# A hybrid attention and linear-attention decoder step: one pass reordered by output column, ACT's results stored from ACT's queue, split weights stored later, one more raw weight slot, bias set-up four steps sooner

## The chip, the cores and the metric

The kernel runs on one core of a Trainium2 chip. The metric is the device time of one execution in microseconds. The engines are named as in the profile: PE multiplies matrices (PEld is its weight load), DVE, ACT and POOL do elementwise work, and SP here does nothing but issue DMAs. ACT and POOL can issue DMAs too. Each engine works through its own queue in order; a wait in a queue holds everything behind it.

## The reference

One layer of a decoder works on 2048 prompt tokens and 64 sample tokens (8 sequences of 8), with a model width of 1024. All data are float32.

```
z = x @ w_in                      # 1024 -> q, k, v, g_att, gq, gk, gv, g_gla, g_lr, r_att, r_gla
o_att = windowed attention(q, k, v) with sinks and a relative bias       # 8 heads, window 128
o_gla = gated linear attention(gq, gk, gv, log_sigmoid(g_lr @ w_gk_up + b_gk))   # 4 heads, chunks of 64
h_att = (o_att * silu(g_att)) @ w_pa          # 512 -> 1024
h_gla = (rmsnorm(o_gla) * silu(g_gla)) @ w_pg # 1024 -> 1024
merged = sigmoid(r_att) * h_att + sigmoid(r_gla) * h_gla
x = layer_norm(ALPHA * x + merged @ w_o)
```

It also returns the last K and V rows and the linear-attention states.

## The kernel before

**Three products for one.** A float32 product is made of three fast ones: each operand is split into a rounded high part and the rest (`split`: ACT casts the high part at L142, DVE subtracts at L143), and PE adds high*high (L1291), high*low (L1292) and low*high (L1293).

**Sets, passes, groups.** The 2112 tokens are cut into three blocks of 704, each of two halves of T = 352. The work of PE is a fixed list of 719 `groups`, in nine sets: x0 (groups 0 to 176), x1 (177 to 351), a0, u0, x2, a1, u1, a2, u2. A set "x" multiplies the input of one token block by all columns of `w_in`; a set "a" is attention's projection `w_pa` (32 groups), a set "u" the projection `w_pg` (32 groups). A pass is a weight with 256 output columns (p); two passes go side by side (j = 0, 1). In the sets x a pass is done by a seven-product scheme on 2x2 blocks (`ORDER`), with sums and differences of weight blocks made by POOL (`tt`, L338). In the sets a and u (`PLAIN`) it is done plainly: a group is `(c, k, t)` for the output column block c, the depth block k and the token half t. A group with `kh` = 4 is 12 matmuls of 128x352, one with `kh` = 2 (the sets a) is 6. The products of the two k of one (c, t) add up in one PSUM bank; with k = 1 the bank is complete and its sink reads it. Four banks (`role`) take turns.

**Weights.** Three helpers run ahead of PE by a number of groups. `w_first` (LR = 8 ahead) has SP load a raw block into a slot of the ring `ws` (9 slots). `w_make` (LM = 4 ahead) has POOL combine blocks where the scheme asks for it, and ACT and DVE split them into a slot of the ring `wp` (6 slots). In x0 four of seven split weights are then stored by SP in DRAM (`wk_d`, L361), and `w_kept` (LK = 5) loads them back in x1 and x2.

**Sinks.** `combine` hands each finished block to the pass's sink. `keep_sink` stores q, k and v (where the block is still in PSUM, ACT copies it first, L186); `silu_sink` the gates; `tanh_sink` (the passes w_ra and w_rg at the end of each set x) has ACT take a tanh (L211) and SP store it (L212); `gated_sink` (sets a) has DVE multiply a block with its gate (L219), which `partners` had SP load (L175, LP = 2 groups ahead), and SP store it (L221). All these tiles come from the ring `fin` (10 slots).

**Side work.** Attention (`att_*`), the linear attention (`gla_*`), the low-rank gate (`gate`, L703) and the set-up of the relative bias (`setup0` to `setup5`) are put between the groups by `at(t, f)`: f is emitted after group t's work, counted in steps of one full group. In this version the bias set-up starts at step 17, its products (`setup1`) come at steps 20, 22, 24 and 26, and the two calls of `gate` in x0 come at steps 22 and 26. `setup3` loads the bias for each phase of attention by eight DMAs (L669).

**Order.** PE's order is the order in which the code emits (a manual schedule). On the other engines a scheduler orders the instructions, except where `issue_after` pins one behind another; so an engine may run ahead of the group list.

Of the kernel before, what the change touches and what calls it, by code (L numbers as in the profile page):

```python
# [12 lines left out]
F32 = mybir.dt.float32  # L13
# [8 lines left out]
P = 128  # L22
# [35 lines left out]
def kernel(ctx, tc, io):  # L58
# [20 lines left out]
    T = MT  # L79

    def mtile(tag, dt=F32, name=None):
        n, bufs = {"xb": (4 * T, 16), "a": (T, 8), "fin": (T, 10), "ws": (512, 9), "wp": (D, 6)}[tag]
        pool = px if tag == "xb" else pr
        return pool.tile([P, n], dt, tag=tag, name=name or tag, bufs=bufs)

# [38 lines left out]
    def at(t, fn):  # L124
        side.setdefault(max(int(t), now[0]), []).append(fn)
# [24 lines left out]
    def later(f):  # L150
        def g():
            with tc.issue_after(pin["a"].ins), tc.issue_after(pin["d"].ins):
                f()
        return g
# [27 lines left out]
    def keep_sink(dst):  # L182
        def f(z, ps, parts, p, c, ts):
            if ps:
                z, src = mtile("fin"), z
                nc.scalar.copy(z, src)  # L186
            nc.sync.dma_start(dst[:, c, ts], z)
            wrote(dst, c, ts)
        return f

# [15 lines left out]
    def tanh_sink(dst):  # L206
        def f(z, ps, parts, p, c, ts):
            src = z
            if ps:
                z = mtile("fin")  # L210
            nc.scalar.activation(z, src, AF.Tanh, scale=0.5)  # L211
            nc.sync.dma_start(dst(2 * p + c, ts), z)  # L212
        return f

    def gated_sink(z, ps, parts, p, c, ts):
# [41 lines left out]
    for n, (kind, s, kh, prs) in enumerate(sets):  # L257
        start_of.append(len(groups))
        base.append(int(tk))
        for pr_ in prs:  # L260
            if not groups:
                for k, t in ((0, 0), (1, 0), (0, 1), (1, 1)):
                    for c in range(2):
                        for j, (q, p) in enumerate(pr_):
                            groups.append((n, q, (c, k, t), s, p, 4 * t + 2 * c + j, False))
            elif seq[n] in PLAIN:
                for c in range(2):
                    for k in range(2):
                        for j, (q, p) in enumerate(pr_):
                            for t in range(2):  # L270
                                groups.append((n, q, (c, k, t), s, p, role[2 * j + t], False))
            elif len(pr_) == 2:
                for i in ORDER:
                    for j, (q, p) in enumerate(pr_):
                        b = role[j] if i in (1, 6, 5, 3) else role[2 + j]
                        groups.append((n, q, i, s, p, b, True))
                role = role[2:] + role[:2]
            else:
                (q, p), = pr_
                r = [role[2], role[3], role[0], role[1]]  # L280
                for j, i in enumerate(ORDER):
                    groups.append((n, q, i, s, p, r[j % 4], False))
                role = [r[3], r[0], r[1], r[2]]
        tk += (len(groups) - start_of[-1]) * kh / 4
# [3 lines left out]
    XS = (X0, X1, X2)  # L288


    raws, wps, acc, parts = {}, {}, {}, {}
    LR, LK, LM, LP = 8, 5, 4, 2
    BLK = {1: (0, 0), 7: (1, 0), 6: (1, 1), 2: (0, 1)}

    def made_here(q, p, s):
# [5 lines left out]
    def w_first(g):  # L301
        n, q, i, s, p, b, ch = groups[g]
        if type(i) is tuple:
            c = None if i[2] else i[:2]
        elif made_here(q, p, s):
            c = BLK.get(i)
        else:
            c = None if i in KEPT else {1: (0, 0), 2: (0, 1), 4: (1, 1)}[i]
        if c is not None:
            t = mtile("ws")[:, :q.kh * P]  # L310
            nc.sync.dma_start(t, q.w[c[0], c[1], p])
            raws[q.name, p, c] = t

    def w_kept(g):
# [5 lines left out]
    def w_make(g):  # L320
# [37 lines left out]
        split(w[:, :m], w[:, m:], src)  # L358
        if i in KEPT and keeps(q, p, s):
            d = wk_d[q.name, p, i] = dram.tile([P, 2 * m], F32, name=f"wk_{q.name}{p}{i}")  # L360
            nc.sync.dma_start(d, w.bitcast(F32))  # L361

    def combine(g, ps):
        n, q, i, s, p, b, ch = groups[g]
# [245 lines left out]

    nbgk = const.tile([P, GH], F32, name="nbgk")
    wgk = const.tile([P, HK], F32, name="wgk")
    at(8, later(consts))

    sink = const.tile([P, NH], F32, name="sink")
# [47 lines left out]
    def setup3():  # L663
        flat = bs_d.rearrange("h q j -> h (q j)")
        for kv in range(2):
            b = w4(name="bias").rearrange("p (g k) -> p g k", g=G)
            for g in range(G):
                f = flat[kv * G + g, 127:127 + P * (LB - 1)].rearrange("(q j) -> q j", j=LB - 1)
                nc.sync.dma_start(b[:, g, :], f[:, :2 * W])  # L669
            st1["bias", kv] = b  # L670

    bias_s = const.tile([P, 2, W + TS], F32, name="bias_s")
# [10 lines left out]
            nc.sync.dma_start(bias_s[32 * b:32 * b + 32], bias_s[:32])  # L683


    at(17, later(setup0))
    for h in range(0, NH, 2):
        at(20 + h, later(lambda h=h: setup1(h)))
    at(20, later(setup2))
    at(29, later(setup4))  # L690
    at(34, setup5)

    def gate_load(B):
        x = B["x"] = mtile("fin", name="gin")
# [124 lines left out]
    def samp_load():  # L819
        for z in [z_kv] + z_q + z_ga:  # L820
            need(z, range(2), NP, NT)
        SA["kv"] = mt("skv", 2 * NS, 1).rearrange("p (a t) -> p a t", a=2)
        SA["kw"] = mt("kw", W, 1)
        nc.sync.dma_start(SA["kv"], z_kv[:, :, NP:])
        nc.sync.dma_start(SA["kw"], z_kv[:, 0, NP - W:NP])
        SA["zq"], SA["sil"] = (mt("zs", G * W, 4, name=n)[:, :G * NS].rearrange("p (g t) -> p g t", g=G) for n in ("szq", "ssl"))
        for j in range(2):
            nc.sync.dma_start(SA["zq"][:, 2 * j:2 * j + 2], z_q[j][:, :, NP:])
            nc.sync.dma_start(SA["sil"][:, 2 * j:2 * j + 2], z_ga[j][:, :, NP:])
        kc = w4(name="kc").rearrange("p (b c) -> p b c", b=NB)  # L830
        vc = w4(name="vc").rearrange("p (b c) -> p b c", b=NB)
        nc.sync.dma_start(kc, io["ck"].rearrange("b w c -> w b c"))
        nc.sync.dma_start(vc, io["cv"].rearrange("b w c -> w b c"))
        SA["kc"], SA["vc"] = kc, vc
        nc.sync.dma_start(io["o_ks"][:, 0:W - TS, :], io["ck"][:, TS:W, :])
        nc.sync.dma_start(io["o_vs"][:, 0:W - TS, :], io["cv"][:, TS:W, :])
# [277 lines left out]
    def samp_a(B):  # L1114
# [7 lines left out]
        nc.gpsimd.memset(qz, 0.0)  # L1122
        for b in range(NB):
            nc.vector.tensor_copy(qz[:, b, b % 4 * TS:(b % 4 + 1) * TS], B["q"][:, Tp + b * TS:Tp + (b + 1) * TS])
        kz = mt("kz", 4 * HK, 1).rearrange("p (b k) -> p b k", b=4)
        nc.vector.tensor_tensor(kz, kdT.unsqueeze(1).broadcast_to([P, 4, HK]),
                                bsel.unsqueeze(2).broadcast_to([P, 4, HK]), ALU.mult)
        B.update(qz=qz, kz=kz)
# [135 lines left out]

    wo = []
    half = 0
    last_ = start_of[U2] + 14
    NG = len(groups)
    for g, (n, q, i, s, p, b, ch) in enumerate(groups):
        if 8 <= g + LR < NG:  # L1270
            w_first(g + LR)
        if g + LK < NG:
            w_kept(g + LK)
        if 8 <= g + LM < NG:
            w_make(g + LM)
        if g + LP < NG:
            _, q_, i_, s_, p_, _, _ = groups[g + LP]
            parts[g + LP] = q_.partners(i_, p_, s_)
        xh, xl = ops[n].op[i[1:] if type(i) is tuple else i]
        w = wps.pop(g)  # L1280
        m = q.kh * P
# [267 lines left out]
```

## Time and profile before

| | |
|---|---|
| three runs | 1844.45, 1842.92, 1842.38 us, median 1842.92 us |
| profiled execution | 1844.21 us, its span 1842.3 us |
| PE busy | 1782.9 us, 97% of the span |
| DVE, ACT, POOL busy | 1062.9 us (58%), 832.6 us (45%), 336.1 us (18%) |
| mean granted TensorE clock | 0.99 |
| data moved | 452.03 MB, 245 GB/s |

PE's busy share says that PE is nearly always at work; what is left is found by cutting the span into stretches and looking at each for PE's idle time and for the granted clock, which falls to half for some microseconds after some of the stalls. The wait lists say on what PE waited, and SP's own list says what the DMAs behind it waited for.

### The profile page before, as it was taken

The page shows a single profiled execution, that of the slowest core. Times are in us where ns is not written, and L with a number is a line of the kernel's source. Part 1 is how long each engine was busy: PE and PEld are TensorE (multiplying, and loading weights), DVE is VectorE, ACT ScalarE, POOL GpSimd, SP SyncE. Part 2 cuts the span into 40 slices and gives each one's busy share as a digit, 9 for nine tenths or more (in the row PEclk, how much of TensorE's full clock was granted, in tenths as well). Part 3 has the DMA queues.
Part 4 walks back from the last instruction along what each step waited for, and adds up shares of the span by engine and source line. Part 5 has one row for each costly group of instructions (what it writes and reads, how often), then busy time and mean ns, then how long its engine had stood idle before and what let it go on. Part 6 is the DMA issues. An engine that isn't in the chain of part 4 may idle for free.

```text
span 1842.3 us, 31141 instructions
## 1 busy us (share of the span) xinstructions
PE 1782.9 (97%) x10850; PEld 1659.2 (90%) x10850; DVE 1062.9 (58%) x2077; ACT 832.6 (45%) x1983; POOL 336.1 (18%) x473
## 2 busy tenths in 40 slices
PE   8989999998999999999899999999999999999997
PEld 7888988998898899999899998899999889998886
DVE  6568676767636554545566446545455544535665
ACT  5747554645835643545334645544445332311100
POOL 4333345454100000000033000000000022021111
PEclk9999999999999999999999999999999999999999
DMA  6689588887698779888886897689888987976531
GB/s 192 237 294 320 196 291 284 299 281 244 201 297 290 239 233 295 274 262 270 285 236 134 274 313 228 218 277 330 264 279 284 299 228 188 293 152 213 159 110 52
DMA packets 291340, 452.03 MB, mean 245 GB/s; under 512 B 29981, under 2 KB 210517, under 8 KB 291168
## 3 DMA queue, kind: packets, MB, share of 16 engines
q1 hardware_dynamic: 283264, 440.61, 72.6%
q0 software_dynamic: 7824, 9.31, 3.6%
q8 instruction: 86, 1.41, 0.3%
q14 instruction: 70, 0.57, 0.1%
q10 hardware_dynamic: 96, 0.13, 0.0%
HBM read 297.52 MB, written 153.30 MB: 245 GB/s over the span
## 4 chain that ended last, share of the span: by engine, by line
PE 71%; DMA 11%; ACT 6%; DVE 5%; issue 3%; POOL 3%; SPq 1%; DVEq 0%; ACTq 0%; POOLq 0%
PE pd L1291 16%; PE pd L1293 16%; PE pd L1292 16%; PE pd L1355 3%; PE pd L1354 3%; PE pd L1356 3%; DMA ws<-w_g 2%; POOL ws L338 2%; DMA r<-ug_d 2%; DVE wp L143 1%; DMA part<-ra_d 1%; PE pa L811 1%; PE pa L765 1%; PE pa L797 1%; PE pa L1085 1%
## 5 line engine op out<-in xcount | busy, mean ns | idle before, releaser
L143 DVE TENSOR_TENSOR wp<-ws,wp 128x512 fp32r<-128x512 f32 (+1 forms) x396 | 271.9, 691 | 216.4 <-ACT wp L142 207.8
L142 ACT CAST wp<-ws 128x512 fp32r<-128x512 f32 (+1 forms) x396 | 233.7, 595 | 222.0 <-PE pd L1293 145.0
L338 POOL TENSOR_TENSOR ws<-ws 128x256 f32<-128x256 f32 x162 | 140.6, 898 | 159.9 <-DVE wp L143 116.0
L1071 POOL TENSOR_SCALAR sq<-sq 128x1 f32<-128x1 f32 x68 | 22.6, 333 | 727.6 <-ACT on L1070 727.6
L374 ACT COPY m<-pd 128x352 f32<-128x352 f32 x146 | 65.6, 453 | 89.2 <-PE pd L1293 89.1
L1291 PE MATMUL pd<-x7h,wp 128*128 128x352 f32 x292 | 97.4, 334 | 4.0 <-ACT wp L142 2.4
L1355 PE MATMUL pd<-woh,x 128*128 128x512 f32 x256 | 100.0, 391 | 0.0
L1354 PE MATMUL pd<-woh,x 128*128 128x512 f32 x256 | 99.8, 390 | 0.0
L1356 PE MATMUL pd<-wol,x 128*128 128x512 f32 x256 | 99.5, 389 | 0.0
L1291 PE MATMUL pd<-x1h,wp 128*128 128x352 f32 x292 | 96.2, 329 | 2.9 <-ACT fin L186 2.3
L1291 PE MATMUL pd<-x2h,wp 128*128 128x352 f32 x292 | 98.7, 338 | 0.0
L1291 PE MATMUL pd<-x6h,wp 128*128 128x352 f32 x292 | 97.5, 334 | 0.9 <-ACT wp L142 0.9
L1291 PE MATMUL pd<-x3h,wp 128*128 128x352 f32 x292 | 97.1, 333 | 0.0
L1291 PE MATMUL pd<-x4h,wp 128*128 128x352 f32 x292 | 96.9, 332 | 0.0
L1291 PE MATMUL pd<-x5h,wp 128*128 128x352 f32 x292 | 96.9, 332 | 0.0
L1293 PE MATMUL pd<-x1h,wp 128*128 128x352 f32 x292 | 94.3, 323 | 1.8 <-DVE wp L143 1.8
L1293 PE MATMUL pd<-x7h,wp 128*128 128x352 f32 x292 | 94.4, 323 | 0.9 <-DVE wp L143 0.7
L1292 PE MATMUL pd<-x2l,wp 128*128 128x352 f32 x292 | 95.0, 325 | 0.0
L1293 PE MATMUL pd<-x5h,wp 128*128 128x352 f32 x292 | 94.9, 325 | 0.0
L1292 PE MATMUL pd<-x5l,wp 128*128 128x352 f32 x292 | 94.9, 325 | 0.0
L1293 PE MATMUL pd<-x2h,wp 128*128 128x352 f32 x292 | 94.7, 324 | 0.0
L1293 PE MATMUL pd<-x6h,wp 128*128 128x352 f32 x292 | 94.4, 323 | 0.1
(441 smaller groups left out, 5271.0 us busy)
## 6 DMA issues: line engine op xcount, KB each, us to landing
wp<-wk_w_g SPq DMA_DIRECT2D x96, 512.0 KB
ws<-w_g SPq DMA_DIRECT2D x120, 256.0 KB
wk_w_g<-wp SPq DMA_DIRECT2D x48, 512.0 KB
wp<-wk_w_ra SPq DMA_DIRECT2D x32, 512.0 KB
wp<-wk_w_rg SPq DMA_DIRECT2D x32, 512.0 KB
ws<-w_at SPq DMA_DIRECT2D x54, 256.0 KB
wp<-wk_w_at SPq DMA_DIRECT2D x24, 512.0 KB
ws<-w_pg SPq DMA_DIRECT2D x48, 256.0 KB
```

Source lines behind the costliest of these rows:

```text
L142: pin["a"] = nc.scalar.copy(dst_h, src)
L143: i = eng.tensor_tensor(dst_l, src, dst_h.bitcast(F32), ALU.subtract)
L338: nc.gpsimd.tensor_tensor(o[:, c], x[:, c], y[:, c], op)
L374: nc.scalar.copy(A[i], ps)
L765: mm(ps[kv][:, j, k0:], A["zq"][r, g0 + j, :], A["kk"][r, 0, k0:], start=True, stop=True, tile_position=(kv * HD, 0))
L1071: nc.gpsimd.tensor_scalar(sq[:n], sq[:n], EPS, None, op0=ALU.add)
L1291: mm(ps, wh, xh[:, ts], start=first, stop=False, skip_group_check=ch)
L1292: mm(ps, wh, xl[:, ts], start=False, stop=False, skip_group_check=ch)
L1293: mm(ps, wl, xh[:, ts], start=False, stop=(k == q.kh - 1 and not (type(i) is tuple and i[1] == 0)), skip_group_check=ch)
L1354: mm(ps, xh[:, xs], hi, start=(k == 0), stop=False)
L1355: mm(ps, xl[:, xs], hi, start=False, stop=False)
L1356: mm(ps, xh[:, xs], lo, start=False, stop=(k == KT - 1))
```

## The change

- **Order of the sets a.** Within one column block c, the pass j is now outside the depth block k: a pass's two k follow each other, four groups to a pass, and its two banks are read while the other pass is at work. The sets u keep their order.
- **Queues.** The stores that follow an ACT instruction (`tanh_sink` always, `keep_sink` where ACT copied from PSUM) are issued from ACT's queue and no longer from SP's.
- **Split weights.** A store of a split weight is emitted one group later and pinned behind the newest raw load on SP.
- **Lead.** One more `ws` slot (10) and one group more of lead for raw loads (LR = 9); in x0 one group more for splitting (LM + 1); for the gates of the sets a four groups more (LP + 4).
- **Space.** One slot fewer for the scheme's intermediate sums (`a`, 7); three tiles of the sample work move into the rings `fin` and `ws`.
- **Bias set-up.** All its steps come four steps sooner (`SU` = 13), and `setup3` loads with one DMA for four heads: two instead of eight.

```diff
-        n, bufs = {"xb": (4 * T, 16), "a": (T, 8), "fin": (T, 10), "ws": (512, 9), "wp": (D, 6)}[tag]
+        n, bufs = {"xb": (4 * T, 16), "a": (T, 7), "fin": (T, 10), "ws": (512, 10), "wp": (D, 6)}[tag]
...
-            nc.sync.dma_start(dst[:, c, ts], z)
+            (nc.scalar if ps else nc.sync).dma_start(dst[:, c, ts], z)
...
             nc.scalar.activation(z, src, AF.Tanh, scale=0.5)
-            nc.sync.dma_start(dst(2 * p + c, ts), z)
+            nc.scalar.dma_start(dst(2 * p + c, ts), z)
...
+                jk = [(j, k) for j in range(2) for k in range(2)]
                 for c in range(2):
-                    for k in range(2):
-                        for j, (q, p) in enumerate(pr_):
-                            for t in range(2):
-                                groups.append((n, q, (c, k, t), s, p, role[2 * j + t], False))
+                    for j, k in jk if kind == "a" else [(j, k) for k, j in jk]:
+                        q, p = pr_[j]
+                        for t in range(2):
+                            groups.append((n, q, (c, k, t), s, p, role[2 * j + t], False))
...
-    LR, LK, LM, LP = 8, 5, 4, 2
+    LR, LK, LM, LP = 9, 5, 4, 2
...
-            nc.sync.dma_start(t, q.w[c[0], c[1], p])
+            pin["r"] = nc.sync.dma_start(t, q.w[c[0], c[1], p])
...
             d = wk_d[q.name, p, i] = dram.tile([P, 2 * m], F32, name=f"wk_{q.name}{p}{i}")
-            nc.sync.dma_start(d, w.bitcast(F32))
+            late.setdefault(g - 3, []).append(lambda: nc.sync.dma_start(d, w.bitcast(F32)))
...
+    SU = 13
...
-            for g in range(G):
-                f = flat[kv * G + g, 127:127 + P * (LB - 1)].rearrange("(q j) -> q j", j=LB - 1)
-                nc.sync.dma_start(b[:, g, :], f[:, :2 * W])
+            f = flat[kv * G:(kv + 1) * G, 127:127 + P * (LB - 1)].rearrange("g (q j) -> q g j", j=LB - 1)
+            nc.sync.dma_start(b, f[:, :, :2 * W])
...
-    at(17, later(setup0))
+    at(SU, later(setup0))
     for h in range(0, NH, 2):
-        at(20 + h, later(lambda h=h: setup1(h)))
-    at(20, later(setup2))
-    at(29, later(setup4))
-    at(34, setup5)
+        at(SU + 3 + h, later(lambda h=h: setup1(h)))
+    at(SU + 3, later(setup2))
+    at(SU + 12, later(setup4))
+    at(SU + 17, setup5)
...
-        SA["kv"] = mt("skv", 2 * NS, 1).rearrange("p (a t) -> p a t", a=2)
-        SA["kw"] = mt("kw", W, 1)
+        SA["kv"] = mtile("fin", name="skv")[:, :2 * NS].rearrange("p (a t) -> p a t", a=2)
+        SA["kw"] = mtile("fin", name="kw")[:, :W]
...
-        kz = mt("kz", 4 * HK, 1).rearrange("p (b k) -> p b k", b=4)
+        kz = mtile("ws", name="kz").rearrange("p (b k) -> p b k", b=4)
...
-        if 8 <= g + LM < NG:
-            w_make(g + LM)
-        if g + LP < NG:
-            _, q_, i_, s_, p_, _, _ = groups[g + LP]
-            parts[g + LP] = q_.partners(i_, p_, s_)
+        while nm < NG and nm <= g + (LM + 1 if groups[nm][3] == 0 and seq[groups[nm][0]] == "x0" else LM):
+            w_make(nm)
+            nm += 1
+        for f in late.pop(g, ()):
+            with tc.issue_after(pin["r"].ins):
+                f()
+        while nq < NG and nq <= g + (LP + 4 if groups[nq][1] is PA_ else LP):
+            _, q_, i_, s_, p_, _, _ = groups[nq]
+            parts[nq] = q_.partners(i_, p_, s_)
+            nq += 1
```

More of the change, by code (lines that the diff above doesn't have):

```diff
@@ L288 @@
     XS = (X0, X1, X2)
-    raws, wps, acc, parts = {}, {}, {}, {}
-    LR, LK, LM, LP = 8, 5, 4, 2
+    raws, wps, acc, parts, late = {}, {}, {}, {}, {}
+    LR, LK, LM, LP = 9, 5, 4, 2
     BLK = {1: (0, 0), 7: (1, 0), 6: (1, 1), 2: (0, 1)}
@@ L1266 @@
     half = 0
-    last_ = start_of[U2] + 14
+    nm, nq = 8, 0
     NG = len(groups)
```

## The prediction

> **What bounds the kernel now.** I read the page first, then the span in stretches, then PE's waits, then SP's own waits, and last the timeline at the stalls.
>
> ```profile
> PE 1782.9 (97%) x10850; PEld 1659.2 (90%) x10850; DVE 1062.9 (58%) x2077; ACT 832.6 (45%) x1983; POOL 336.1 (18%) x473
> ...
> PE 71%; DMA 11%; ACT 6%; DVE 5%; issue 3%; POOL 3%; SPq 1%; DVEq 0%; ACTq 0%; POOLq 0%
> ```
>
> PE is the bound, and the change removes no PE instruction. What it can win is PE's idle time and the time at a low clock. The stretches, cut at the borders of the sets, show where these lie (length, then busy time and instructions of PE, PEld, DVE, ACT, POOL, then clock, DMA share, GB/s):
>
> ```profile
> 0.00:40.00 40.00, 32.84 (x180) 31.45 (x180) 23.09 (x33) 20.63 (x35) 22.08 (x40) 1.00 0.67 214
> 40.00:100.00 60.00, 57.72 (x320) 48.65 (x321) 36.85 (x55) 41.34 (x83) 16.30 (x20) 0.91 0.62 217
> 100.00:135.00 35.00, 29.69 (x190) 26.84 (x189) 20.98 (x42) 16.48 (x45) 13.22 (x16) 1.00 0.91 309
> ...
> 232.00:302.00 70.00, 64.25 (x394) 61.69 (x393) 51.82 (x92) 37.36 (x88) 33.80 (x43) 1.00 0.81 279
> 302.00:400.00 98.00, 93.45 (x578) 90.07 (x577) 64.07 (x126) 55.07 (x135) 45.82 (x62) 1.00 0.86 297
> 400.00:490.00 90.00, 82.24 (x510) 76.92 (x509) 66.70 (x114) 54.75 (x124) 41.68 (x52) 0.96 0.70 229
> 490.00:878.00 388.00, 387.39 (x2440) 368.85 (x2438) 202.34 (x415) 196.80 (x492) 13.41 (x30) 1.00 0.83 268
> 878.00:924.00 46.00, 40.65 (x230) 39.08 (x229) 25.46 (x56) 15.94 (x39) 2.88 (x6) 0.93 0.89 287
> 924.00:1423.00 499.00, 497.93 (x3259) 470.79 (x3258) 269.45 (x577) 243.95 (x591) 49.02 (x85) 1.00 0.81 257
> 1423.00:1465.00 42.00, 38.97 (x232) 37.45 (x231) 26.40 (x67) 16.50 (x42) 4.87 (x9) 0.96 0.94 304
> ...
> 1545.00:1590.00 45.00, 41.45 (x247) 36.97 (x246) 24.57 (x55) 14.19 (x31) 1.93 (x4) 0.96 0.86 263
> ```
>
> Loss of a stretch = (length - PE busy) + (1 - clock) x length. 40:100 loses 2.3 + 5.4 = 7.7; 100:135 5.3; 232:302 5.8; 302:400 4.6; 400:490 7.8 + 3.6 = 11.4; the sets a: a0 (878:924) 5.4 + 3.2 = 8.6, a1 (1423:1465) 3.0 + 1.7 = 4.7, a2 (1545:1590) 3.6 + 1.8 = 5.4. The sets x1 and x2 (490:878, 924:1423) lose 0.6 and 1.1 us: there nothing can be won. So some 35 us lie in x0 behind its start, 18.7 in the sets a. One group of 12 matmuls takes 12 x 387.39/2440 = 1.9 us, one of the sets a 0.95.
>
> PE's and then SP's waits (total, times, longest):
>
> ```profile
> PE pd L1291 <- DVE fin L219: 8.1, 6, 2.6
> ...
> PE pd L1291 <- ACT wp L142: 4.0, 4, 1.4
> ...
> PE pa L703 <- ACT brow L652: 2.1, 1, 2.1
> ...
> PE pa L751 <- DMA kk<-z_kv: 1.5, 1, 1.5
> ```
> ```profile
> SPq L311 <- DVE wp L143: 127.1, 76, 11.3
> SPq L212 <- ACT fin L211: 78.2, 56, 5.6
> ...
> SPq L361 <- DVE wp L143: 59.8, 37, 4.9
> ...
> SPq L187 <- ACT fin L186: 33.8, 13, 8.0
> ```
>
> SP's list is the key: one in-order queue carries the loads that PE will need and the stores that wait for ACT and DVE. In 232:302, SP, then the chain from the load on:
>
> ```profile
> 223.20 0.42 SPq L311 DMA_DIRECT2D ws<-w_g  x1
> 228.60 0.32 SPq L361 DMA_DIRECT2D wk_w_g<-wp  x1
> ...
> 233.19 0.59 SPq L311 DMA_DIRECT2D ws<-w_g  x1
> ```
> ```profile
> 233.19 4.75 DMA ws<-w_g
> 238.76 1.24 POOL ws L338 x2
> ...
> 245.58 0.63 ACT wp L142
> ```
>
> From 223.6 to 228.6 SP does nothing but wait to store a split weight; the raw load behind it goes out at 233.19, POOL combines until 245.6, and ACT's split is what PE waits for.
>
> **The change, part by part.**
>
> *Order of the sets a, and their gates earlier.* PE's costliest wait is for DVE's gate product (8.1 us), which waits for the gate's load. Loads of parts and the stall at a0's start:
>
> ```profile
> 894.36 3.76 DMA part<-ra_d
> ...
> 909.31 5.93 DMA part<-ra_d
> ```
> ```profile
> 880.63 0.32 PE L1292 MATMUL pd<-x(0, 0)_9663,wp 128*128 128x352 f32 x1
> 880.79 0.32 PE L1293 MATMUL pd<-x(0, 0)_9663,wp 128*128 128x352 f32 x1
> ...
> 882.38 0.46 ACT L211 ACTIVATE fin<-pd 128x352 f32<-128x352 f32 x1
> ...
> 882.74 0.39 ACT L142 CAST wp<-ws 128x256 fp32r<-128x256 f32 x1
> ...
> 882.89 0.48 PE L1291 MATMUL pd<-x(0, 1)_9705,wp 128*128 128x352 f32 x1 [1.78 <-ACT fin L211]
> ...
> 883.17 0.49 PE L1292 MATMUL pd<-x(0, 1)_9705,wp 128*128 128x352 f32 x1
> ```
>
> A part takes 3.8 to 5.9 us and is issued two groups (1.9 us) ahead; its bank is wanted again 3 groups after its last matmul. With six groups (5.7 us) of lead and, by the new order, 5 groups until the bank is wanted, both gaps are covered. The bank of 882.89 is the last one of x1 to be emptied; in the new order it is wanted two groups (1.9 us) later, as long as the stall (1.78). Behind the stall the matmuls start about 0.29 us apart instead of 0.16: the clock's share of the loss goes with the stall. What is late next is ACT behind a load (a1). I take 7 of 8.6 in a0, 1.5 of 4.7 in a1, 4 of 5.4 in a2: -12.5; bounds 0 and -18.7. The x tiles of k = 1 are wanted two groups sooner; should they be late, 2 x 0.95 us in each of three sets is added (5.7), which I leave to the range.
>
> *SP relieved: ACT's stores moved, split weights stored behind the next raw load, more lead.* 112 us of SP's waits for ACT (78.2 + 33.8) leave the loads' queue, and the 59.8 for the stores of split weights come behind the load instead of ahead of it. Where these waits cost PE is x0. I take 4 of 5.8 in 232:302, 3 of 5.3 in 100:135, 1 of 4.6 in 302:400, 4 of 11.4 in 400:490, and 1.5 at x0's start, where SP's longest wait (8.0 for ACT's copy) stands: -13.5; bounds 0 and -29, nearer the middle since POOL's and ACT's own chains (233 to 245) stay.
>
> *Set-up four steps sooner.* Now the last bias product meets `gate` at step 26, and PE waits 2.1 us for ACT's copy of the row; half clock of about 10.8 us in 40:100 (5.4 lost) belongs to this and to the wait at step 14. Moved, that product comes with the first `gate` at step 22, as another does now without a long wait, and step 26 has the gate alone. But steps 13 to 16 now stand where x0's first sinks empty PE's spare banks: a new wait as long as the old one is possible. I take -4; bounds -5.5 and +5.5. What set-up's other instructions cost (POOL's DMAs, ACT's and DVE's casts) stays the same and lies four steps earlier beside PE's 7.6 us; SP's small bias stores and loads move out of its densest stretch.
>
> *Bias in two DMAs.* Two for eight saves six issues of the median below ahead of the load of `kk`, 2.6 us; PE's wait for that load is 1.5. I take -1.5; bounds 0 and -2.6.
>
> ```profile
> L669 SPq DMA_DIRECT2D bias<-bs_d x24: 319/430/1057, 100.5 to 1072.6; - x24
> ```
>
> *ACT pays.* By the code 96 tanh stores and 39 of copies, 135, now stand in ACT's queue: each waits for ACT's own result and holds what is behind it, a split or a bank's copy. Prices (ns, least/median/greatest), SP's today and ACT's two at the end:
>
> ```profile
> L212 SPq DMA_DIRECT2D ra_d<-fin x48: 319/320/1605, 339.0 to 1352.1; - x48
> ```
> ```profile
> L1410 ACTq DMA_DIRECT2D o_y<-z x2: 370/384/397, 1836.2 to 1836.9; - x2
> ```
>
> 0.38 plus some 0.07 for ACT's result to end (an estimate: the ACT row of 882.38 lasts 0.46 and the next starts 0.36 later, which leaves 0.1 at most) is 0.45 x 135 = 61 us of ACT. ACT is busy 833 us, of which the chain holds 6% of 1842 = 110, or 13%: +8. Bounds 0 (ACT is idle 55%) and +61 (all on the chain); nearest is the chain's share.
>
> *Stores of split weights hold their `wp` slot longer*, by a group (1.9 us) and SP's wait for the raw load. The slot is refilled about five groups before its use, so I take +1; bounds 0 and +8 (1.9 us in each of x0's four stretches that lose time). *One slot fewer of `a`* (six live at a time), *three tiles moved into `fin` and `ws`* (x2 and later, which lose 1 us), *a longer lead of splits in x0* (its slots still wait for PE): 0; if their cover fails, ACT or DVE waits one group, 1.9 us, at each.
>
> Sum: -12.5 - 13.5 - 4 - 1.5 + 8 + 1 = -22.5. The profiled execution took 1844.21 us, so 1821.7; the median run is 1.29 lower: 1820.
>
> Some 10 us of this are clock: 3.2 + 1.8 in a0 and a2, some 3 in 40:100 and 2 in 400:490. The trace shows half clock right behind a stall of 1.78 us, so I count it with the stalls. The Trainium skill (TensorE: Matmul & The Clock Gate, Part 1) says that the clock falls after at least one idle window of about 3.4 us. By that rule a stall of 1.78 us costs its own length alone and the sum is -12.5; here the row and the page differ, and the row decides.
>
> **The rivals.**
>
> *Only the sets a gain.* In x0 the weights would be late because the transfers are slow, not because SP issues late. For it: the DMA share of 0.91 in 100:135, and 4.75 us for a raw load. Against it: the 5 us in which SP stood still at 223 to 228. Then -12.5 for the sets a, -1.5 for the bias and half of ACT's cost, +4, give -10: 1834.2 profiled, 1833 in the median. The Trainium skill (DMA: Bandwidth & Descriptors, Issuing engines are not separate DMA queues) says that issuing from several engines saves only the sequencer's time of issue; that rule speaks for this rival, since it gives nothing for what waits in a queue.
>
> *The low clock stays.* If the half-clock stretches hang on something else than these stalls, the idle time comes back alone: -22.5 + 10 = -12.5, or 1830 in the median. Against it: 882.89, where the slow matmuls start right behind the gap.
>
> *Slower: ACT becomes the queue that blocks.* [...] If ACT's 61 us of issues came onto the chain for more than half (31 us eat the whole gain), the kernel would be slower; with 0.65 of them, 40 us, it takes 1851. Against it: x1 and x2, with 2/3 of these stores, lose 1 us today and have ACT half idle.
>
> *No change.* Gain and ACT's cost cancel by chance: 1843.
>
> **How the numbers follow.** The forecast, 1806 to 1830, has 0.55; the low clock staying 0.07; the sets a alone, up to 1839, 0.16; no change 0.08; slower 0.12; a gain over 38 us 0.02. Below 1804 and above 1846 lie some 0.15 together, so the range is 1804 to 1846. A difference under 0.2% (3.7 us) can't be told from none here. Faster 0.55 + 0.07 + 0.16 + 0.02 = 0.8, same 0.08, slower 0.12. The forecast's own range is 1806 to 1830.
>
> **What would show it.** PE's wait for DVE L219 falls from 8.1 us to under 2, and a0's stretch is fully busy at clock 1.00. L212 appears in ACT's queue with about 0.4 us each. SP has no wait for ACT L211, and the wait of 5 us ahead of a raw load near 223 is gone. No wait of L703 for L652. x0 ends some 12 us sooner. It is wrong if PE's waits for ACT's splits grow in 302:490, if a new half clock appears near 45 us, or if new waits for `wp` slots stand in x0.

## The result, and the profile after

The changed kernel takes 1818.6 us, median of 6 runs (1813.76 to 1821.71), against 1845.13 (1842.38 to 1850.44, 6 runs) before: ratio 0.9853, 95% interval 0.9832 to 0.9874. The forecast was 1820. The profiled execution took 1816.59 us with a span of 1814.8, 27.5 less than before's 1842.3. Two executions in the experiments below, one of the new order with the short lead and one with ACT's tiles stored by SP, ran at a granted clock of 0.56 and 0.75 and took 2915 and 2176 us; the medians and ratios leave them out.

The page after, its part on engines and its part on the chain:

```profile
PE 1768.1 (97%) x10850; PEld 1654.2 (91%) x10850; DVE 1059.9 (58%) x2077; ACT 837.0 (46%) x1983; POOL 334.0 (18%) x473
...
PE 71%; DMA 11%; ACT 4%; DVE 4%; issue 4%; POOL 3%; SPq 1%; ACTq 0%; DVEq 0%; POOLq 0%
```

PE issues the same 10850 matmuls and is busy 14.8 us less. A matmul at the low clock lasts longer, and the mean clock rose from 0.990 to 0.994: (0.010 x 1842.3) - (0.006 x 1814.8) = 7.5 us. The rest of the 14.8 is left unexplained. The other 12.7 us of the gain are idle time of PE (59.4 before, 46.7 after). ACT's busy time hardly moves although 135 issues were added to its queue: issues are not counted as busy, and the price of ACT's stores cannot be read from this line.

The span after in stretches, cut at the same matmuls as the prediction's stretches of x0 (0, 44.2, 100.0, 135.1, 232.1, 302.6, 400.1 and 490.0 before), then at the first matmul of each set. Columns: length, busy time and instructions of PE, PEld, DVE, ACT, POOL, then clock, DMA share, GB/s.

```profile
0.00:41.50 41.50, 34.64 (x212) 31.44 (x212) 29.68 (x36) 20.75 (x35) 24.17 (x40) 1.00 0.66 226
41.50:95.10 53.60, 49.89 (x293) 45.91 (x290) 32.00 (x52) 41.18 (x82) 15.58 (x20) 0.97 0.70 233
95.10:124.90 29.80, 28.51 (x189) 26.96 (x188) 21.83 (x43) 16.57 (x45) 12.62 (x16) 1.00 0.96 345
...
222.50:286.70 64.20, 63.41 (x397) 62.25 (x397) 49.69 (x90) 36.84 (x86) 31.92 (x41) 1.00 0.89 306
286.70:384.00 97.30, 93.49 (x574) 91.40 (x573) 65.35 (x126) 55.96 (x134) 45.82 (x62) 0.98 0.86 296
384.00:474.20 90.20, 82.19 (x509) 77.43 (x509) 65.62 (x114) 55.59 (x124) 41.31 (x52) 0.96 0.69 229
...
861.70:900.40 38.70, 36.80 (x227) 35.70 (x226) 23.18 (x54) 18.86 (x45) 2.37 (x6) 1.00 0.96 319
900.40:974.40 74.00, 72.84 (x458) 71.69 (x457) 45.29 (x82) 24.31 (x52) 25.53 (x37) 1.00 0.78 205
...
1399.70:1439.80 40.10, 38.24 (x234) 36.42 (x233) 27.58 (x71) 18.48 (x47) 3.19 (x7) 1.00 0.99 317
1439.80:1522.90 83.10, 79.96 (x493) 75.33 (x492) 38.18 (x91) 24.70 (x57) 19.79 (x31) 0.98 0.75 199
1522.90:1560.50 37.60, 36.70 (x233) 33.51 (x232) 18.80 (x43) 9.65 (x22) 1.66 (x3) 1.00 0.90 286
```

The same sets before, a0, u0, a1, u1, a2, cut in the same way:

```profile
878.00:923.60 45.60, 40.25 (x227) 38.68 (x226) 25.16 (x56) 15.79 (x38) 2.66 (x6) 0.93 0.89 287
923.60:996.20 72.60, 72.60 (x459) 71.69 (x457) 44.17 (x78) 25.90 (x54) 26.99 (x38) 1.00 0.77 199
...
1421.60:1464.00 42.40, 39.37 (x233) 37.82 (x232) 26.68 (x68) 17.04 (x44) 4.59 (x9) 0.96 0.94 303
1464.00:1545.40 81.40, 79.37 (x495) 74.37 (x493) 39.36 (x96) 25.67 (x59) 19.83 (x30) 1.00 0.79 213
1545.40:1588.20 42.80, 39.25 (x233) 34.79 (x232) 22.65 (x50) 13.08 (x29) 1.66 (x3) 0.96 0.86 262
```

The cut at 490.0 (474.2 after) lies inside x1, whose first matmul starts at 461.1 before and 446.8 after: x0 itself is 14.3 us shorter. Up to the later cut it is 15.8 us, in three places: 4.9 in the first two stretches (100.0 to 95.1), 5.3 in the third (35.1 to 29.8), 6.3 in 222:287 (70.5 to 64.2). From 287 on nothing is won (97.5 to 97.3, 89.9 to 90.2). The sets a give 6.9 + 2.3 + 5.2 = 14.4; u0 and u1 give back 1.4 + 1.7. Of the 2.7 us in the very first stretch, 2.1 come without any change to x0: in the kernel before with only the sets a changed (below) it takes 42.1.

PE's waits after (total, times, longest):

```profile
PE pd L1297 <- ACT fin L186: 5.0, 3, 3.7
...
PE pa L1086 <- DVE sg L1103: 4.6, 3, 3.6
PE pa L1086 <- ACT gv L1054: 3.7, 2, 3.4
PE pa L1086 <- ACT on L1074: 3.1, 1, 3.1
PE pd L1297 <- DVE fin L219: 2.4, 3, 1.2
...
PE pd L1297 <- ACT fin L211: 1.9, 2, 1.1
```

The gate's wait for DVE L219 fell from 8.1 to 2.4, the waits for ACT's splits (4.0) and for `brow` (2.1) are gone. What leads now is other work of ACT and DVE: the sinks' copies, and the products of the chunk scan (`gv`, `sg`, `on`).

SP's waits after:

```profile
SPq L312 <- DVE wp L143: 122.0, 79, 11.3
SPq L319 <- PE pd L1299: 100.3, 73, 5.6
...
SPq L362 <- DVE wp L143: 68.7, 31, 8.3
```

The two waits for ACT's tiles (78.2 + 33.8) are gone. The wait to store split weights is not shorter (68.7 against 59.8). SP now waits longer for PE, at the loads of kept weights, L319: 100.3 against 71.6 (then L318). A load that waits because its slot is still in use by PE goes out as early as the slot allows; in a queue of loads that wait is no loss of its own. The place where SP stood still for 5 us ahead of a raw load, after:

```profile
218.69 0.38 SPq L312 DMA_DIRECT2D ws<-w_g  x1
219.16 0.40 SPq L362 DMA_DIRECT2D wk_w_g<-wp  x1
...
221.91 0.54 SPq L312 DMA_DIRECT2D ws<-w_g  x1
222.88 0.33 SPq L362 DMA_DIRECT2D wk_w_g<-wp  x1
```

Each raw load (L312) now goes out ahead of the store of a split weight (L362), and SP's pauses between 218 and 228 are shorter than 2.5 us. ACT's new issues, from the rows of its tanh store:

```profile
L212 ACTq DMA_DIRECT2D ra_d<-fin x48: 326/326/537, 323.6 to 1330.3; - x48
```

With the other 48 tanh stores (`rg_d`, the same median) and the copies' 39 (326 to 332) that is 135 x 0.326 = 44 us of ACT's queue.

### The profile page after: what moved, and what is told of

The parts are those of the page before. It is cut to its first block, busy times and chain, and to the rows that moved or that the text cites. A ratio compares the mean times of both kernels' runs of the same rounds, so it can differ in the third digit from the quotient of the medians.

```text
span 1814.8 us, 31047 instructions
## 1 busy us (share of the span) xinstructions
PE 1768.1 (97%) x10850; PEld 1654.2 (91%) x10850; DVE 1059.9 (58%) x2077; ACT 837.0 (46%) x1983; POOL 334.0 (18%) x473
## 4 chain that ended last, share of the span: by engine, by line
PE 71%; DMA 11%; ACT 4%; DVE 4%; issue 4%; POOL 3%; SPq 1%; ACTq 0%; DVEq 0%; POOLq 0%
PE pd L1297 17%; PE pd L1299 16%; PE pd L1298 16%; PE pd L1361 3%; PE pd L1360 3%; PE pd L1362 3%; POOL ws L339 2%; DMA part<-ra_d 2%; DMA ws<-w_g 1%; DMA r<-ug_d 1%; PE pa L812 1%; DMA mg_d<-fin 1%; PE pa L798 1%; PE pa L1086 1%; PE pa L766 1%
## 5 line engine op out<-in xcount | busy, mean ns | idle before, releaser
L339 POOL TENSOR_TENSOR ws<-ws 128x256 f32<-128x256 f32 x162 | 141.5, 908 | 157.0 <-DVE wp L143 93.7
L1297 PE MATMUL pd<-x2h,wp 128*128 128x352 f32 x292 | 97.9, 335 | 0.0
L1297 PE MATMUL pd<-x3h,wp 128*128 128x352 f32 x292 | 97.8, 335 | 0.0
L1297 PE MATMUL pd<-x6h,wp 128*128 128x352 f32 x292 | 97.3, 333 | 0.0
L1298 PE MATMUL pd<-x1l,wp 128*128 128x352 f32 x292 | 94.8, 325 | 0.0
L1299 PE MATMUL pd<-x3h,wp 128*128 128x352 f32 x292 | 94.8, 325 | 0.0
L1298 PE MATMUL pd<-x3l,wp 128*128 128x352 f32 x292 | 94.7, 324 | 0.0
```

Of the source, the lines that this page charges most:

```text
L339: nc.gpsimd.tensor_tensor(o[:, c], x[:, c], y[:, c], op)
L1297: mm(ps, wh, xh[:, ts], start=first, stop=False, skip_group_check=ch)
L1298: mm(ps, wh, xl[:, ts], start=False, stop=False, skip_group_check=ch)
L1299: mm(ps, wl, xh[:, ts], start=False, stop=(k == q.kh - 1 and not (type(i) is tuple and i[1] == 0)), skip_group_check=ch)
```

## The experiments

Each takes one part out of the changed kernel, puts one part alone into the kernel before, or alters one suspected cost. The theory they test is the prediction's sum: parts that add. The rival is that they interact. Differences in us are differences of the ratios to the kernel before, times 1845.1; a ratio's interval is about 0.002 (3.5 us) to each side, so a difference between two of these kernels is uncertain by some 5 us. The stretches of the profiled executions say where a difference lies (us, cut at the first matmul of each set; one execution of each kernel):

| kernel | x0 | x1 | a0 + a1 + a2 | u0 + u1 |
|---|---|---|---|---|
| before | 461.1 | 416.9 | 130.8 | 154.0 |
| before, sets a alone | 459.9 | 418.2 | 111.0 | 159.8 |
| before, ACT's stores alone | 456.6 | 417.7 | 126.4 | 151.7 |
| changed | 446.8 | 414.9 | 116.4 | 157.1 |
| changed, old order | 446.4 | 417.4 | 128.0 | 150.8 |
| changed, short lead of parts | 447.4 | 418.6 | 129.8 | 156.9 |
| changed, old order and short lead | 446.9 | 416.9 | 128.0 | 151.1 |
| changed, ACT's tiles stored by SP | 459.7 | 415.0 | 111.7 | 159.3 |
| changed, split weights stored at once | 452.5 | 418.4 | 115.0 | 153.6 |
| changed, shorter lead of weights | 454.5 | 417.7 | 116.4 | 153.2 |
| changed, set-up at step 17 | 450.1 | 417.4 | 117.5 | 156.9 |
| changed, bias in eight DMAs | 448.0 | 416.6 | 117.5 | 156.1 |
| changed, ACT's stores halved | 455.7 | 421.0 | 119.7 | 152.4 |
| changed, ACT stores in token set 0 alone | 443.5 | 417.6 | 112.1 | 155.1 |

Five of these kernels have the x0 of the changed kernel, and it takes 443.5 to 447.4 us in them. u1 alone takes from 78.1 us (shorter lead of weights) to 84.1 (sets a alone): a stall of the scan comes and goes there, whatever was tested.

**The sets a.** The old order of the sets a in the changed kernel:

```diff
-    for j, k in jk if kind == "a" else [(j, k) for k, j in jk]:
+    for j, k in [(j, k) for k, j in jk]:
```

> The changed kernel with the old order in the sets a (k outside j); the lead of six groups for the gates stays. Theory (order and lead each cover a part of the stalls): the wait for the last bank of x1 comes back, 1.8 us with 1.7 us of half clock behind it, and some waits for DVE L219; a0 about 4 us longer than in the changed kernel, all three sets a together 5 to 7, the time 1824. Rival (the lead alone does it): the sets a stay as short as they are, 1819. x0 ends within 1 us of the changed kernel's either way.

1824.63 us, ratio 0.9894 (0.9875 to 0.9913): 7.6 more. The time is the theory's, its parts are not: the sets a are 11.6 us longer, not 5 to 7, and u0 and u1 are 6.3 shorter. The short lead of the parts with the new order kept:

```diff
-    while nq < NG and nq <= g + (LP + 4 if groups[nq][1] is PA_ else LP):
+    while nq < NG and nq <= g + LP:
```

> The changed kernel with the gates of the sets a loaded two groups ahead again; the new order stays. Theory: a part takes 3.8 to 5.9 us and is issued 1.9 us ahead, the new order leaves five groups (4.8 us) until the bank is wanted, together 6.7 us, so only the slow ones are late: 2 to 4 us more over the three sets, 1821. Rival (the order alone does it): 1819. Other rival (the lead is what counts): most of the 14 us that the sets a gained is lost, 1830.

1834.24 us, 0.9936 (0.992 to 0.9952): 15.3 more, beyond the other rival's 1830 and far beyond the theory's 1821. Both undone:

> The changed kernel with the old order of the sets a and their gates two groups ahead: both undone. Alone, the order is worth some 7.5 us and the lead some 15. Theory (both cover the same lateness of a gate, so together they are worth less than their sum): the sets a take as long as before the change, 45.6 + 42.5 + 42.8, 14.6 us more than now, 1833 to 1835. Rival (they cover different waits and add): 1841.

1824.07 us, 0.9888 (0.9871 to 0.9904): 6.5 more, which misses both expectations on the other side. For the sets a alone the theory of overlapping parts was about right (11.6 us more, where it had 14.6): with the old order, with the short lead, and with both undone they take 128.0, 129.8 and 128.0 us, and 116.4 in the changed kernel. So neither part alone shortens them; only the two together do. The three times differ elsewhere, u0 and u1 above all. DVE's wait for the parts shows what each does alone, in the kernel before, in both undone, and with the new order and the short lead:

```profile
DVE fin L219 <- DMA part<-ra_d: 20.0, 13, 3.5
```
```profile
DVE fin L219 <- DMA part<-ra_d: 17.1, 14, 4.3
```
```profile
DVE fin L219 <- DMA part<-ra_d: 32.5, 21, 4.6
```

With the old order and the long lead the parts come in time (DVE waits 0.5 us), but PE still waits 7.3 us for L219 and 4.1 for L211: the old order wants the banks too soon. With the new order and the short lead DVE waits longest. SP and DVE in its a0:

```profile
884.03 0.93 SPq L175 DMA_DIRECT2D part<-ra_d  x2
...
888.98 0.80 SPq L221 DMA_DIRECT2D mg_d<-fin  x2
889.83 0.91 SPq L175 DMA_DIRECT2D part<-ra_d  x2
```
```profile
888.43 0.97 DVE L219 SCALAR_TENSOR_TENSOR fin<-part,pd 128x352 f32<-128x352 f32 x2 [4.14 <-DMA part<-ra_d]
```

A pair of parts goes out at 884.03, DVE has them at 888.43, SP stores the products (L221) at 888.98, and only behind these stores, in the same queue, does the next pair go out, at 889.83. One round takes 5.8 us. The new order asks for a pair every four groups, 4 x 0.95 = 3.8 us, the old one for four parts in eight groups. With six groups of lead a part is asked for before those stores, and DVE's wait is 6.4 us in the changed kernel. The order pays only with the lead, and the lead only with the order.

Both put into the kernel before, alone:

> The kernel before, with the new order of the sets a and the six groups of lead for their parts, and nothing else. Prediction's term: 12.5 us less, 1832.5. Theory from undoing both in the changed kernel (6.5 us): 1838.5, with the sets a shorter by some 14 us together and part of it given back in u0 and u1, where a stall of ACT's late products grows by as much. Rival: x0's stalls do not depend on this, so the sets a gain as in the changed kernel and nothing is given back: 1831.

1830.99 us, 0.9924 (0.9906 to 0.9941): 14 less. The rival has the time, by luck, and not the account: more than 14 was won, and part of it was given back, as the theory had it. Its sets a and u, in the order a0, u0, a1, u1, a2:

```profile
878.10:914.70 36.60, 36.45 (x226) 35.78 (x226) 22.46 (x51) 15.14 (x38) 2.56 (x6) 1.00 0.96 308
914.70:990.40 75.70, 73.05 (x458) 71.62 (x457) 45.26 (x82) 25.75 (x54) 26.01 (x36) 1.00 0.81 213
...
1416.90:1454.90 38.00, 37.80 (x233) 36.46 (x232) 25.67 (x65) 16.14 (x42) 4.33 (x9) 1.00 0.95 313
1454.90:1539.00 84.10, 81.89 (x495) 76.95 (x493) 39.40 (x95) 25.86 (x59) 19.56 (x29) 0.96 0.82 218
1539.00:1575.40 36.40, 36.40 (x232) 33.51 (x231) 20.60 (x46) 11.14 (x25) 1.66 (x3) 1.00 0.90 272
```

Without ACT's stores the sets a are free of PE's idle time but for 0.4 us, 19.8 us shorter than before, and 3.1 + 2.7 come back in u0 and u1. In u0 it is one wait of 2.4 us of the chunk scan's matmul (L1062) for DVE's state `S`, in u1 one of 2.2 (L1145 for ACT's `on`): I read this as PE coming sooner to a step of the scan that keeps its own pace; no run tests it.

**SP's queue.** ACT's tiles stored from SP again:

```diff
-    (nc.scalar if ps else nc.sync).dma_start(dst[:, c, ts], z)
+    nc.sync.dma_start(dst[:, c, ts], z)
...
-    nc.scalar.dma_start(dst(2 * p + c, ts), z)
+    nc.sync.dma_start(dst(2 * p + c, ts), z)
```

> The changed kernel with all stores issued from SP again; split weights are still stored late. Theory (SP's waits for ACT delay raw loads in x0, ACT pays less for the issues than SP gains): x0 ends 5 us later than in the changed kernel, the sets a some 2 us longer because the gates queue behind the stores of the tanh tiles, 1825. Rival 1 (ACT pays as much as SP gains): 1819. Rival 2 (ACT pays more): faster than the changed kernel, 1812.

1829.28 us, 0.9915 (0.9897 to 0.9933): 11.4 more. SP's waits for ACT's tiles are back (81.7 us for L211, 34.8 for L186), and its waits for DVE's splits (L312 and L362) are less, 123.2 us against 190.7: the waits stand one behind the other. x0 is 12.9 us longer than in the changed kernel, where the theory had 5, spread over all stretches from 41 to 398, 2.4 to 3.7 us in each. It is hardly shorter (459.7) than with the sets a's change alone (459.9): without the moved stores the other parts bring x0 next to nothing. The sets a, which the theory had 2 us longer, are shorter: a0 and a1 by 1.8 and 2.7. Split weights stored at once:

```diff
-    late.setdefault(g - 3, []).append(lambda: nc.sync.dma_start(d, w.bitcast(F32)))
+    nc.sync.dma_start(d, w.bitcast(F32))
```

> The changed kernel with split weights stored as soon as they are made (by the group count), not pinned behind the newest raw load. Theory: SP waits again for DVE's split ahead of raw loads; x0 ends 4 to 6 us later, with PE's waits for ACT and DVE of wp between 220 and 300 back, 1823. Rival (the moved ACT stores and the larger lead cover it already): 1819.

1823.98 us, 0.9884 (0.9866 to 0.9903): 5.7 more. The size is the theory's, and x0 is 5.7 longer, but not where the theory had it. The loss lies between 41 and 231 (57.0, 32.7 and 99.6 us against 53.6, 29.8 and 97.6; 2.4 come back at x0's end); the stretch behind it, the prediction's 232:302, takes 64.5 against 64.2. SP's wait for the splits that it stores, L362, is 103.8 us instead of 68.7, and PE waits for `kk` again (1.8 us). The shorter lead of raw loads and splits in x0:

```diff
-    LR, LK, LM, LP = 9, 5, 4, 2
+    LR, LK, LM, LP = 8, 5, 4, 2
...
-    while nm < NG and nm <= g + (LM + 1 if groups[nm][3] == 0 and seq[groups[nm][0]] == "x0" else LM):
+    while nm < NG and nm <= g + LM:
```

> The changed kernel with the old lead of raw loads (8 groups) and of splits in x0 (4); the ring of raw slots keeps its 10. Theory (SP's queue order is what mattered, the lead follows it): x0 1 to 2 us longer, 1820. Rival (the lead carries x0's gain, since loads and splits start a group, 1.9 us, sooner): x0 6 us longer, 1825. The sets a within 1 us of the changed kernel's.

1827.69 us, 0.9904 (0.9888 to 0.9919): 9.4 more, the rival, with x0 7.7 longer and the sets a the same. PE's wait for ACT's splits, gone in the changed kernel, is back (6.8 us) and larger than before the change (4.0). 4.9 of x0's 7.7 lie in the prediction's 232:302, which takes 69.1 us instead of 64.2. Which of the two leads carries this, that of the raw loads or that of the splits, was not separated.

The bias set-up at step 17 again:

```diff
-    SU = 13
+    SU = 17
```

> The changed kernel with the bias set-up at its old steps (17 on). In the changed kernel PE still loses 5.3 us between 82 and 89 us, now on ACT's copy of a finished block (3.87) instead of on the bias row. Theory (the gate's work on ACT is what PE runs into there, whatever stands beside it; the wait moved and little was won): x0 within 2 us of the changed kernel's, 1819 to 1821. Rival (the prediction's: the wait for the bias row at step 26 and its half clock come back): x0 4 us longer, 1823.

1823.79 us, 0.9878 (0.986 to 0.9897): 4.6 more, no more than such a difference is uncertain by, with x0 3.3 longer. And not where the prediction had it: PE does not wait for `brow`, and the second stretch (40 to 94 here) takes 53.7 us, as in the changed kernel, 53.6. The loss is 3.1 us in the stretch 124 to 225, where PE's matmuls of the attention (L752) wait 3.6 us for copies of ACT and DVE. How the set-up's place leads to these was not pursued.

The bias in eight DMAs again:

```diff
-    f = flat[kv * G:(kv + 1) * G, 127:127 + P * (LB - 1)].rearrange("g (q j) -> q g j", j=LB - 1)
-    nc.sync.dma_start(b, f[:, :, :2 * W])
+    for g in range(G):
+        f = flat[kv * G + g, 127:127 + P * (LB - 1)].rearrange("(q j) -> q j", j=LB - 1)
+        nc.sync.dma_start(b[:, g, :], f[:, :2 * W])
```

> The changed kernel, with the bias loaded in eight DMAs for a token set again instead of two. Prediction's term: 1.5 us, so 1820.1; the wait of L752's matmul for kk is longer by about 1.5 us. Rival: the load of kk is not behind these loads any more since set-up moved forward by four steps, and nothing changes: 1818.6. Rival: the eight small loads hold raw weights back in SP's queue in x0: 1822 or more.

1819.65 us, 0.9867 (0.9846 to 0.9889): 2.6 more by the ratios, 1.1 by the medians, which cannot be told from nothing. PE does not wait for `kk` in it, so the wait of 1.5 us that is gone was not won by the two DMAs.

ACT's stores alone, in the kernel before (the edit is the reverse of the one that gave them back to SP):

> The kernel before, with nothing changed but that ACT issues the stores of its own 135 tiles. Theory: the parts work alike alone and together; undone in the changed kernel this part cost 11.5 us, so it gives 1845 - 11.5 = 1833.5 here. Rival (queues in series): SP still waits to store the split weights at once, 59.8 us of waits, so the loads go out hardly sooner, while ACT pays its 13 us all the same: 1840 to 1848. Rival: SP's relief from these stores is the larger part of the whole gain and stands alone: under 1830.

1837.75 us, 0.9968 (0.9952 to 0.9983): 5.9 less, some half of what the same part is worth in the changed kernel, and between the theory and its first rival. By the times the two worths (5.9 and 11.4) are not clear of each other; in x0 they are, 4.5 against 12.9 us. The rival's mechanism is seen: SP's waits for ACT's tiles (112 us) are gone, but those for DVE's splits grew from 127.1 + 59.8 to 172.5 + 77.3, by 63 us.

**ACT's price.** Every one of the 135 stores in two halves, both issued by ACT (the tanh stores here, the copies' in the same way):

```diff
-    nc.scalar.dma_start(dst(2 * p + c, ts), z)
+    for o in (0, T // 2):
+        nc.scalar.dma_start(dst(2 * p + c, slice(ts.start + o, ts.start + o + T // 2)), z[:, o:o + T // 2])
```

> The changed kernel with each of the 135 stores that ACT issues cut into two of half the columns, both issued by ACT: same bytes, twice the issues. Theory of the prediction (ACT pays 0.45 us a store, and 13% of that lands on PE's path): about 0.38 x 135 = 51 us more of ACT's queue, of which 7 us show, 1825. Rival 1 (ACT's queue has room wherever these stand): 1819. Rival 2 (the stores stand where ACT is PE's releaser, at the ends of the sets x): more than half shows, 1845.

1831.85 us, 0.993 (0.9912 to 0.9949): 14.2 more, twice the theory. By the medians of their rows the halves take 96 x 0.334 + 96 x 0.332 + 24 x 0.358 + 24 x 0.344 + 18 x 0.396 + 12 x 0.445 = 93 us in all against 44: 49 us more of ACT's queue, and 14.2 / 49 = 29% of that reach the end. PE's two waits that grew most:

```profile
PE pa L1091 <- ACT gv L1059: 11.3, 5, 4.5
PE pa L538 <- ACT fin L186: 5.5, 1, 5.5
```

In the changed kernel the same two were 3.7 and 1.9. But the largest of them do not stand behind issues. Of the 14.2 us, 6.7 lie in the first stretch (48.2 us against 41.5), with the wait of 5.5; ACT had been idle for 6.58 us ahead of it, waiting for POOL:

```profile
42.28 0.62 ACT L142 CAST wp<-ws 128x512 fp32r<-128x512 f32 x1 [6.58 <-POOL ws L344]
42.80 0.45 ACT L186 COPY fin<-pa 128x352 f32<-128x352 f32 x1
```

One of POOL's operations there lasts 5.58 us by the trace, where in the changed kernel none of L339 takes over 1.6; why is not known. The longest wait for `gv` (4.5) stands behind a split too, as it does in the changed kernel (3.4), and the next (3.7) is there in the changed kernel as well, put down to `sg` (3.6). Of the five only one of 0.4 us has issues just ahead of it in ACT's queue. The price per issue cannot be had from this run; halving also doubles the number of transfers.

**A version that keeps the gain and leaves a part of the price.** ACT issues its stores in token set 0 alone:

```diff
-    (nc.scalar if ps else nc.sync).dma_start(dst[:, c, ts], z)
+    (nc.scalar if ps and ts.start < 2 * T else nc.sync).dma_start(dst[:, c, ts], z)
...
-    nc.scalar.dma_start(dst(2 * p + c, ts), z)
+    (nc.scalar if ts.start < 2 * T else nc.sync).dma_start(dst(2 * p + c, ts), z)
```

> The changed kernel, with ACT issuing its stores only in token set 0 (x0, a0's and u0's own stores are not ACT's); in the sets x1 and x2 the same stores go out from SP again. Theory: the stores in ACT's queue pay where SP's queue is what PE waits for, in x0, and cost where it is not: with all stores back on SP the sets x1, a0, u0, x2, a1, u1 and a2 took 2.5 us less together than in the changed kernel. So about 1816 us in the median, against 1818.6 for the changed kernel; x0 as long as there (442 us), a0 and a1 shorter by 2 us each. Rival: those 2.5 us are chance alignments of stalls (u1 has one of 5 us that comes and goes), and the time is 1818 to 1822. Rival: SP's waits for ACT's copies hold weights back in x1 and x2 too: over 1823.

1813.58 us, median of 4 runs (1809.95 to 1814.91), 0.9827 (0.9805 to 0.985): 4.8 less than the changed kernel. The intervals of the two ratios overlap a little and the two were not timed side by side, so it is probably the fastest of all, not certainly. Its a0 and a1 (its profiled execution is its fastest run):

```profile
861.10:897.60 36.50, 36.48 (x227) 35.81 (x226) 22.25 (x51) 15.42 (x39) 2.42 (x6) 1.00 0.97 317
...
1397.30:1434.70 37.40, 37.40 (x234) 36.50 (x233) 23.36 (x60) 15.10 (x36) 3.28 (x7) 1.00 0.95 310
```

PE has no idle time in either, where the changed kernel has 1.9 us in each. The expected 2 us per set came: a0 and a1 are 2.2 and 2.7 shorter. In this one execution x0 is also 3.3 shorter and x1 2.7 longer, which the edit does not explain.

## Why the prediction was right, and where its steps were not

The sum, -22.5, stands against -26.5 of the medians, and the time itself was met within 2 us, the nearer because this before is 2.2 us slower than the one that the forecast started from. The two large terms, the sets a and SP's relief, have the right cause and about the right size. That the sum is so near is partly luck: a term of 4 us did not come, one put at 0 is worth 9.4, and the terms do not add. Of the signs named, two failed narrowly: PE's wait for DVE L219 fell to 2.4 us, not under 2, and a0 keeps 1.9 us of idle time.

- *Sets a: -12.5.* Measured in the stretches -14.4, less 3.1 given back in u0 and u1; alone in the kernel before -14. The mechanism holds, and more strictly than I had it: the two gaps must be covered both, for order or lead alone leaves the sets a at 128 to 130 us. The step that the stall at a0's start goes because the bank is wanted two groups later failed in part: 1.9 us of waits for ACT L211 remain there, and they are gone in both kernels that take ACT's stores out of x1. The give-back in u0 and u1, by the chunk scan, was not in the prediction.
- *SP relieved: -13.5.* By stretch: 100:135 gave 5.3 (3 forecast, and 1.5 of the bias), 232:302 gave 6.3 (4), 302:400 0.2 (1), 400:490 -0.3 (4). The last is the failed term. I counted its 11.4 us as weights that SP loads late, but its waits before and after are for ACT's `gv`, `mg` and `on`, products of the scan; and from 461.1 on the stretch is x1. The longest, for `gv` (2.7 before, 3.4 after), is a late weight after all, but by POOL. ACT after:

```profile
428.00 0.62 ACT L142 CAST wp<-ws 128x512 fp32r<-128x512 f32 x1 [1.74 <-POOL ws L339]
428.52 0.47 ACT L1054 COPY gv<-pa 128x384 f32<-128x384 f32 x1
```

  Before, the same split waits the same 1.74 us for POOL, which in both kernels stood idle for 8 us ahead; what it waited for there is not settled. PE's waits by stretch would have said that the term was not SP's; I read that list for the whole span only. In 232:302 the gain came, but not by the store at 223.6 to 228.6 that I named. The raw load right behind that store went out at 229.48; the one at 233.19, from which I followed the chain, stood behind six other transfers. And with split weights stored at once the stretch is as short as in the changed kernel (64.5 against 64.2), with the shorter lead it is 69.1, with ACT's tiles stored by SP 67.1.
- *A longer lead of raw loads and splits: 0.* Wrong: without it 9.4 us are lost and the wait for ACT's splits is back. I took the slots as the limit, and the lead counted although they were.
- *Parts that add.* Wrong as a form. Undone singly, the moved stores, the late stores, the lead and the set-up lengthen x0 by 12.9 + 5.7 + 7.7 + 3.3 = 29.6 us, although it gained 14.3 in all; put in alone, the moved stores shorten it by 4.5. SP's lists show them in series in one queue: where one wait goes, a part of it comes back as another (63 of 112 us with the stores alone). A weight comes sooner only when all that stands ahead of it has gone.
- *Set-up sooner: -4.* The first two stretches gained 4.9, against 5.5 with the 1.5 at x0's start, but 2.1 of that come without the change. Undoing it costs 4.6, at the edge of what can be told, and elsewhere. The new wait that I thought possible did come. ACT, then PE, in the changed kernel:

```profile
78.06 1.70 ACT L713 ACTIVATE zg<-zg 128x352 f32<-128x352 f32 x4
79.78 1.28 ACT L715 ACT_TABLE_LOAD   x1
...
83.26 1.28 ACT L194 ACT_TABLE_LOAD   x1
...
85.46 0.44 ACT L186 COPY fin<-pd 128x352 f32<-128x352 f32 x1
```
```profile
85.96 0.66 PE L1297 MATMUL pd<-x7h,wp 128*128 128x352 f32 x1 [3.71 <-ACT fin L186]
```

  The copy that empties PE's bank stands behind a whole `gate` with two table loads of 1.28 us: 3.71 us and a half clock behind it, in the place of the wait for `brow` (2.1) and its half clock.
- *Bias: -1.5.* Not told from nothing; the wait for `kk` left with SP's relief.
- *ACT pays: +8.* Open. The time in the queue was smaller (44 us, not 61). What it costs shows only in a0 and a1, which are 4.5 and 4.9 us shorter together in the two kernels where ACT leaves x1's and x2's stores to SP. The doubled stores would give 29% of 44, 13 us, but their largest stalls have other causes, so that neither this nor the chain's 13% is shown.
- *Late stores hold their slot: +1; ring of `a`, tiles in `fin` and `ws`: 0.* PE's waits for DVE's split fell, and x1 and x2 kept their lengths: no sign of a cost.

Of the rivals, "only the sets a gain" fell when SP stored ACT's tiles again: x0 depends on SP by 12.9 us. The Trainium skill (DMA: Bandwidth & Descriptors, Issuing engines are not separate DMA queues) says that issuing from several engines saves only the time of issue. No run here tells that time apart from the waiting: the move took some 43 us of issues (135 x 0.32) and 112 us of waits for ACT out of SP's queue. "The low clock stays" fell: the clock gave its 7.5 us of the 27.5, where 10 were counted. "ACT blocks" is seen in a0 and a1, far below the 40 us that it needed (which would give 1852, not 1851).

## What to carry to other kernels

When loads and stores share an in-order queue, do not add up the gains of clearing it part by part: look for everything that stands ahead of the late load, and expect the first part alone to bring half or less, as here. A store moved to a compute engine's queue paid here where the loads' queue was late (x0), and cost elsewhere (a0, a1); try it first in the stages where PE's waits end in a load. A wait list names only the last releaser: look one row up before calling a wait that engine's own. Read PE's waits stretch by stretch before putting a stretch's idle time down to one cause, and shift an order and the lead of its loads together, because the order sets how many loads one round trip must serve. Name where an undone part should cost time, and look there: three runs here met a forecast time with the loss or gain in another place.

## What the hardware showed

The length of one stall does not say whether the clock falls. PE has the same stall ahead of the same 32 matmuls in the kernel before (L532) and in the kernel before with the sets a alone (L533):

```profile
40.08 4.22 PE L532 MATMUL pa<-r,wg 128*32 128x352 f32 x32 [1.99 <-ACT fin L186]
```
```profile
39.64 2.57 PE L533 MATMUL pa<-r,wg 128*32 128x352 f32 x32 [2.48 <-ACT fin L186]
```

Behind 1.99 us of idle time the 32 matmuls took 4.22 us, behind the longer 2.48 they took 2.57 (clock 0.96 and 1.00 in their first stretches); in the changed kernel 1.92 us had no fall behind it either. So a part of the gain at x0's start is the clock's and not the change's. In the changed kernel the waits of 3.71 us at 85.96 and 3.1 at 1481 did bring it down (0.97 and 0.98 in their stretches). Up to the last set, each fall in the clock records of these traces lasts 3.41 us or twice that. What else decides was not tried.
